# Masked softmax on one core: contiguous first halves, a new order of the last masks and divides, and batch 14 stored in two parts

## The chip, the cores and the metric

The kernel runs on one core of one Trainium2 chip. The metric is the device time of one execution in microseconds (us). All executions quoted here ran at a granted clock of 1.0. Differences of a few tenths rest on several rounds and carry a 95% interval.

## The reference

For each of 16 batches (8 heads x 256 queries = 2048 rows of 256 float32), softmax over the first `length` columns; the others are zero. Lengths are drawn between 128 and 255.

```python
for b in range(batch):
    length = lengths[b]
    masked = x[b, :, :, :length].copy()
    masked = masked - np.max(masked, axis=-1, keepdims=True)
    exp_masked = np.exp(masked)
    result[b, :, :, :length] = exp_masked / np.sum(exp_masked, axis=-1, keepdims=True)
```

## The kernel before

A batch is 2 MB, held as 128 partitions x 16 rows x 256 columns; eight batches have a slot in SBUF. VectorE masks a batch by a minimum in place, ScalarE takes exponentials with row sums, VectorE divides each half (8 of the 16 rows of every partition), the sync queue (SP) stores. Batches 0 to 3 are loaded whole by SP; batches 4 to 15 by GpSimd (POOL), cut to the batch's length rounded up to one of twelve widths.

```python
x_f = x.rearrange("b h q k -> b (h q) k").rearrange("b (p t) k -> b p t k", p=P)
...
for h in range(2):                                    # batch 0, in halves
    s = slice(h * half, (h + 1) * half)
    nc.sync.dma_start(out=xt[:, 0, s], in_=x_f[0, :, s]).then_inc(s_ld[h], 16)
for b in range(1, ahead):                             # batches 1 to 3
    nc.sync.dma_start(out=xt[:, b], in_=x_f[b]).then_inc(s_ld[b + 1], 16)

nc.sync.wait_ge(s_exp, 3)
for b in range(batch):
    s_b = s_st[b % 2]
    for s in parts(b):
        nc.sync.wait_ge(s_out, 2 * b + (s.stop - 1) // half + 1)   # divided
        if b >= 2 and s.start == 0:
            nc.sync.wait_ge(s_b, 64 * (b // 2 + 1))                # store b-2 has landed
        nc.sync.dma_start(
            out=out_f[b, :, s, :], in_=xt[:, b % slots, s, :]
        ).then_inc(s_b, 16 * ((s.stop - s.start) // quarter))
...
for b in range(batch):                                # VectorE
    first = b == 0 or b >= ahead
    if first:
        divide(b, 0)
    if b + 1 < batch:
        mask(b + 1, slice(0, nt))
    if not first:
        divide(b, 0)
    divide(b, 1)
```

Each half of batch 0 is thus 128 pieces of 8 KB at a pitch of 16 KB in memory. Batches 13 and 14 are stored in one piece of 2 MB, batch 15 in two of 1 MB.

The softmax here doesn't subtract the row's maximum and nothing guards it: scores larger than these inputs give would overflow.

## Time and profile before

| | before |
|---|---|
| median of 3 runs | 156.60 us (156.06 to 156.62) |
| span of the profiled run | 154.7 us |
| VectorE busy, ScalarE busy | 75%, 68% |
| 16 transfer engines busy, both queues | 97.9% |
| bytes moved | 62.08 MB, 401 GB/s over the span |
| traffic, start of the first load packet to start of the last packet | 2.1 to 152.7 us |

A line of the view by stretches gives the stretch (us from the start), its length, the busy time of five engines with their number of instructions, then the granted clock, the mean busy share of the 16 transfer engines, and GB/s. It counts a packet whole in the stretch in which the packet starts, so that a share can pass 1. A line of the timeline gives start, duration, engine, source line, operation, tiles, and in brackets how long the engine had been idle and for whom. A line of the waits gives who waited for whom: total us, times, longest. The lines of this kernel stand in the prediction.

### The profile page before, as it was taken

What the parts mean: (1) busy time and instruction counts of PE and PEld (TensorE: products, weight loads), DVE (VectorE), ACT (ScalarE), POOL (GpSimd) and SP (SyncE); (2) the same over time, 40 slices, a digit from 0 to 9 for tenths busy, and PEclk for the clock granted to TensorE, in tenths of its full rate; (3) what the DMA queues carried; (4) which work ended last, traced back from release to release, by engine and by line L of the source; (5) the groups of instructions that cost most, each with busy time, mean ns of one, the idle gap of its engine ahead of it and who ended that gap; (6) DMA issues with size and microseconds to landing.
All of it is one profiled execution on the core that took longest, in us unless ns stands there. A gap on an engine that the chain in (4) does not pass through costs nothing.

```text
span 154.7 us, 1324 instructions
## 1 busy us (share of the span) xinstructions
PE 0.2 (0%) x1; PEld 0.1 (0%) x1; DVE 115.7 (75%) x84; ACT 105.2 (68%) x514; POOL 19.0 (12%) x25
## 2 busy tenths in 40 slices
PE   0000000000000000000000000000000000000000
PEld 0000000000000000000000000000000000000000
DVE  1249999952999696979979696969689629796700
ACT  3087799992692959778695959595976906959200
POOL 4910031000220110201111020202001000000000
DMA  4999999999999999999999999999999999999992
GB/s 116 426 449 424 428 398 406 398 407 447 400 410 395 402 409 414 415 417 411 404 424 407 417 408 409 415 416 416 416 417 419 419 448 415 426 445 419 430 421 85
DMA packets 9988, 62.08 MB, mean 401 GB/s; under 512 B 850, under 2 KB 946, under 8 KB 6274
## 3 DMA queue, kind: packets, MB, share of 16 engines
q1 hardware_dynamic: 5904, 41.95, 65.8%
q0 software_dynamic: 4080, 20.12, 32.1%
q14 instruction: 2, 0.02, 0.0%
q10 hardware_dynamic: 2, 0.00, 0.0%
HBM read 28.51 MB, written 33.55 MB: 401 GB/s over the span
## 4 chain that ended last, share of the span: by engine, by line
DMA 55%; DVE 19%; ACT 8%; issue 8%; ACTq 2%; SPq 1%; POOLq 1%; DVEq 0%
DMA xt<-in_x_dram 34%; DMA out_dram<-xt 21%; DVE xt L222 9%; DVE xt L195 9%; ACT xt L252 8%; ACTq L252 2%; DVE inv_sum L219 1%; SPq L109 1%; POOLq L99 0%; SPq L111 0%; SPq L120 0%; DVEq L212 0%; POOLq L135 0%; POOLq L130 0%; ACTq L247 0%
## 5 line engine op out<-in xcount | busy, mean ns | idle before, releaser
L252 ACT ACTIVATE xt<-xt x256 | 102.4, 401 | 37.2 <-DVE xt L195 37.2
L222 DVE TENSOR_TENSOR xt<-xt,inv_sum 128x2048 f32<-128x2048 f32 x32 | 73.4, 2292 | 1.1
L252 ACT ACTIVATION_READ_ACCUMULATOR xt<-xt x256 | 47.9, 187 | 0.0
L195 DVE SCALAR_TENSOR_TENSOR xt<-down,len_s,xt 128x2048 f32<-128x2048 f32 (+1 forms) x17 | 37.8, 2222 | 13.1 <-DMA xt<-in_x_dram 13.0
L130 POOL DMA_DIRECT2D xt<-in_x_dram x12 | 12.8, 1064 | 95.5 <-issue 50.6
L219 DVE RECIPROCAL inv_sum<-row_sum 128x8 f32<-128x8 f32 x32 | 6.3, 198 | 14.4 <-ACT xt L252 14.4
L149 POOL MEMSET xt<- 128x1536 f32 x4 | 5.3, 1386 | 1.1 <-DVE len_s L186 1.1
L244 ACT ACT_TABLE_LOAD x1 | 1.3, 1283 | 1.6 <-SPq L81 1.6
L178 DVE TENSOR_SCALAR down<-iota_i 128x256 f32<-128x256 int32 x1 | 0.3, 297 | 1.6 <-POOL iota_i L141 1.6
L183 DVE CAST len_b<-word 1x16 bf16<-1x16 int32 x1 | 0.2, 163 | 0.4 <-DMA word<-in_lengths_dram 0.4
L186 DVE TENSOR_SCALAR len_s<-len_f 128x16 f32<-128x16 f32 x1 | 0.2, 174 | 0.3 <-PE len_f L165 0.3
L141 POOL IOTA iota_i<- 128x256 int32 x1 | 0.3, 331 | 0.6 <-SPq L81 0.6
L146 POOL MEMSET seed<- 1x1 f32 x2 | 0.3, 162 | 0.0
L244 ACT ACTIVATE warm<-const-float32-0.0 128x1 f32<-128x1 f32 x1 | 0.2, 203 | 0.0
L144 POOL MEMSET ones<- 1x128 bf16 x1 | 0.2, 194 | 0.0
L165 PE MATMUL len_f<-len_b,ones 1*128 1x16 bf16 x1 | 0.2, 164 | 2.6 <-DVE len_b L183 2.6
L275 POOL MEMSET const-float32-0.0<- 128x1 f32 x1 | 0.1, 98 | 0.3 <-issue 0.3
L165 PEld LDWEIGHTS len_f<-len_b,ones 1*128 1x128 bf16 x1 | 0.1, 99 | 2.6 <-POOL ones L144 2.6
L275 POOL MEMSET const-float32-1.0<- 128x1 f32 x1 | 0.1, 98 | 0.0
L275 POOL MEMSET const-bfloat16-1.0<- 128x1 bf16 x1 | 0.1, 98 | 0.0
L275 POOL MEMSET const-uint8-127<- 128x1 uint8 x1 | 0.1, 98 | 0.0
L275 POOL BASE_LOAD x1 | 0.0, 17 | 0.1
## 6 DMA issues: line engine op xcount, KB each, us to landing
out_dram<-xt SPq DMA_DIRECT2D x19, 1024.0 KB
out_dram<-xt SPq DMA_DIRECT2D x14, 512.0 KB
xt<-in_x_dram SPq DMA_DIRECT2D x3, 2048.0 KB, 16.1
out_dram<-xt SPq DMA_DIRECT2D x3, 2048.0 KB
xt<-in_x_dram POOLq DMA_DIRECT2D x3, 1728.0 KB, 16.9
xt<-in_x_dram POOLq DMA_DIRECT2D x2, 2048.0 KB, 18.5
xt<-in_x_dram POOLq DMA_DIRECT2D x2, 1600.0 KB, 16.8
xt<-in_x_dram POOLq DMA_DIRECT2D x2, 1280.0 KB, 14.8
```

What stands on the lines that cost most here:

```text
L109: nc.sync.dma_start(out=xt[:, 0, s], in_=x_f[0, :, s]).then_inc(s_ld[h], 16)
L130: nc.gpsimd.dma_start(out=xt[:, slot, :, :w], in_=x_n[:, n, :, :w]).then_inc(s_sw[par], 16)
L141: nc.gpsimd.iota(iota_i, pattern=[[1, seq_k]], base=0, channel_multiplier=0).then_inc(s_iota, 1)
L146: nc.gpsimd.memset(seed[:, par : par + 1], 0.0).then_inc(s_st[par], 64)
L149: nc.gpsimd.memset(xt[:, b, :, low:], 0.0).then_inc(s_fill, 1)
L165: nc.tensor.matmul(len_f, lhsT=ones, rhs=len_b, start=True, stop=True).then_inc(s_lenf, 1)
L195: return nc.vector.scalar_tensor_tensor(out=t, in0=down[:, None, lo:hi].to_broadcast([P, s.stop - s.start, hi - lo]), scalar=len_s[:, b : ...
L219: step(nc.vector.reciprocal(out=inv_sum[:, b, s], in_=row_sum[:, b, s]))
L222: nc.vector.tensor_tensor(out=t, in0=t, in1=inv_sum[:, b, s, None].to_broadcast([P, half, seq_k]), op=ALU.mult,).then_inc(s_out, 1)
L244: nc.scalar.activation(out=warm, in_=nc.const_aps.tensor(0.0, (P, 1), F32), func=EXP)
L252: ins = nc.scalar.activation(out=e, in_=e, func=EXP, accum_out=sum_h[:, bass.ds(i, 1), j])
L275: nc = _bacc.Bacc("TRN2", target_bir_lowering=False, num_devices=1)
```

## The change

It means to make the first loads quicker (each half of batch 0 one contiguous megabyte), to let the divide of 13's second half go ahead while VectorE waits for batch 14's load, to have the last mask done before the divides of 14 so that ScalarE isn't kept waiting for it, and to start batch 14's store half a batch earlier.

```diff
+    x_0 = x[0].rearrange("h q k -> (h q) k").rearrange("(u p t) k -> p u t k", u=2, p=P)
+    out_0 = out[0].rearrange("h q k -> (h q) k").rearrange("(u p t) k -> p u (t k)", u=2, p=P)
...
-        elif b < 13 or b == batch - 1:
+        elif b != batch - 3:
             cuts = [0, half, nt]
...
-            nc.sync.dma_start(out=xt[:, 0, s], in_=x_f[0, :, s]).then_inc(s_ld[h], 16)
+            nc.sync.dma_start(out=xt[:, 0, s], in_=x_0[:, h]).then_inc(s_ld[h], 16)
...                                        (batch 0 is stored to out_0 to match)
-            first = b == 0 or b >= ahead
-            if first:
-                divide(b, 0)
-            if b + 1 < batch:
-                mask(b + 1, slice(0, nt))
-            if not first:
-                divide(b, 0)
-            divide(b, 1)
+            at = 0 if b == batch - 2 else 2 if b == batch - 3 else 1 if b == 0 or b >= ahead else 0
+            for h in range(3):
+                if h == at and b + 1 < batch:
+                    mask(b + 1, slice(0, nt))
+                if h < 2:
+                    divide(b, h)
```

More of the change, by code (lines that the diff above doesn't have):

```diff
@@ L119 @@
                     nc.sync.wait_ge(s_b, 64 * (b // 2 + 1))
-                nc.sync.dma_start(
-                    out=out_f[b, :, s, :], in_=xt[:, b % slots, s, :]
-                ).then_inc(s_b, 16 * ((s.stop - s.start) // quarter))
+                if b == 0:
+                    to = out_0
+                    at = xt[:, b, s, :].rearrange("p (u t) k -> p u (t k)", u=2)
+                else:
+                    to = out_f[b, :, s, :]
+                    at = xt[:, b % slots, s, :]
+                nc.sync.dma_start(out=to, in_=at).then_inc(s_b, 16 * ((s.stop - s.start) // quarter))
         def pick(v, n, slot, par, ws):
```

## The prediction

> **What bounds the kernel now.** I read, in this order, the first two parts of the page, its DMA queues, the stretches of the span at the start and the end, the waits of the store queue, and the timeline of the last 28 us. The lines of the page:
>
> ```profile
> PE 0.2 (0%) x1; PEld 0.1 (0%) x1; DVE 115.7 (75%) x84; ACT 105.2 (68%) x514; POOL 19.0 (12%) x25
> ...
> DMA  4999999999999999999999999999999999999992
> GB/s 116 426 449 424 428 398 406 398 407 447 400 410 395 402 409 414 415 417 411 404 424 407 417 408 409 415 416 416 416 417 419 419 448 415 426 445 419 430 421 85
> ...
> q1 hardware_dynamic: 5904, 41.95, 65.8%
> q0 software_dynamic: 4080, 20.12, 32.1%
> ```
>
> No compute engine is above 75% of the span, while the 16 transfer engines are at nine tenths or more in every slice but the first and the last. The two queues' shares add up to 97.9%. The bytes are 62.08 MB; nothing in the change alters them. Traffic runs from 2.0 us to 152.7 us, so 62.08 MB / 150.7 us = 412 GB/s. The time is that stretch, plus 2.0 us ahead of the first packet, plus 2.0 us after the last one (the span is 154.7 us), plus 1.7 us between the span and the timed 156.37 us of the same run. A change therefore gains only where it (a) starts the traffic sooner or makes it denser, (b) fills a hole in it, or (c) shortens the run-out. The chain of waits puts 55% on DMA, but much of its rest is compute that merely lies beside busy queues, so I don't size the change from it.
>
> The stretches at the two ends (us, engines' busy time, granted clock, DMA share, GB/s):
>
> ```profile
> 147.00:147.50 0.50, 0.00 (x0) 0.00 (x0) 0.00 (x0) 0.00 (x0) 0.00 (x0) 1.00 0.89 377
> 150.50:151.00 0.50, 0.00 (x0) 0.00 (x0) 0.00 (x0) 0.00 (x0) 0.00 (x0) 1.00 1.04 442
> 151.25:151.50 0.25, 0.00 (x0) 0.00 (x0) 0.00 (x0) 0.00 (x0) 0.00 (x0) 1.00 0.55 229
> 151.75:152.00 0.25, 0.00 (x0) 0.00 (x0) 0.00 (x0) 0.00 (x0) 0.00 (x0) 1.00 0.24 98
> 152.50:152.75 0.25, 0.00 (x0) 0.00 (x0) 0.00 (x0) 0.00 (x0) 0.00 (x0) 1.00 0.08 33
> ```
>
> The queues are full to 151.25 us; then three or four of the 16 engines run on alone for 1.4 us at the same pace each (98 GB/s at a share of 0.24, 0.24 x 16 = 3.8 engines, 26 GB/s each; all 16 at 430 GB/s are 27 each). So the end belongs to the slowest engines, and their pace does not depend on what the others do.
>
> The last vector instructions and the last load's issue and landing time:
>
> ```profile
> 126.58 2.35 DVE L195 SCALAR_TENSOR_TENSOR xt<-down,len_s,xt 128x2048 f32<-128x2048 f32 x1 [3.29 <-DMA xt<-in_x_dram]
> 137.56 0.42 ACT L252 ACTIVATE xt<-xt  x1 [1.88 <-DVE xt L195]
> 144.33 2.29 DVE L222 TENSOR_TENSOR xt<-xt,inv_sum 128x2048 f32<-128x2048 f32 x1
> ```
> ```profile
> xt<-in_x_dram POOLq DMA_DIRECT2D x1, 2048.0 KB, 17.6
> ```
>
> Counting the instructions back from the end, 126.58 is the mask of 14, 129.08 the second divide of 13, 132.75 the first of 14, 134.97 the mask of 15, 137.46 the second divide of 14, 141.13 and 144.33 the divides of 15. ScalarE idles 1.88 us waiting for the mask of 15, and VectorE 3.29 us before the mask of 14. The last load was issued at 116.06 us and landed 17.6 us later, at 133.7.
>
> The store queue's waits, from 135 to 140 us and from 140 to 144 us:
>
> ```profile
> SPq L119 <- DMA out_dram<-xt: 4.5, 1, 4.5
> SPq L120 <- DVE xt L222: 1.0, 1, 1.0
> ```
> ```profile
> SPq L119 <- DMA out_dram<-xt: 3.6, 1, 3.6
> ```
>
> Its issues are at 133.81 (store 13), 139.78 (14), 143.77 (first half of 15) and 146.65 us (second half). Stores 13 and 15 wait for an older store to land (each waits for the store two batches back), store 14 for store 12 and then 1.0 us more for its divide, and only the very last half for compute alone.
>
> **What the Trainium skill says.** *DMA: Bandwidth & Descriptors*, "Where 436 GB/s comes from", puts the ceiling of one core's 16 ports at 435 GB/s; the plain loads here run at 430 GB/s from 9 to 20 us, so there is hardly anything above them. The same page, "Queues, rings and completion order", says that each engine goes round its queues packet by packet; the trace agrees: from 126 to 128 us both queues pass 36 packets, and the one with the larger packets takes 69% of the time. The same page, "Latency and other measured facts", tells of a slow row pitch from 512 KiB upward. Batch 0's halves have a pitch of 16 KiB, far below that; the trace neither shows nor excludes a small effect at this pitch. *HBM Reference*, "Specifications", says that a core streaming alone is bounded by its 16 DMA engines, which is what the run-out above shows.
>
> **The change part by part.**
>
> *Batch 0's halves contiguous.* Each half is still 128 pieces of 8 KB; only the pitch goes from 16 KB to 8 KB. The stretches of 1 us show 180, 319, 401 and 410 GB/s from 2 to 6 us. Against 430 that is 250 + 111 + 29 + 20 = 410 KB short, or 0.95 us. The 250 KB of the first microsecond are start-up (every engine's first packet, with the share already at 0.87), which the pitch does not touch; I leave them. The remaining 160 KB are 0.37 us, the most that better addresses can give back. Nothing shows that the pitch is the cause: the second half, at the same old pitch, runs at 442 and 492 GB/s. I choose half of it, **0.2 us**. It would go through in full, since the queues are busy ever after.
>
> *Store 0* becomes 256 pieces of 8 KB in place of 128 of 16 KB, and batch 14's two halves likewise, with 16 completion packets more: 128 + 128 + 16 = 272 packets, 17 per engine. From 134 to 146 us packets of 8 and 16 KB together moved 5.26 MB in 12 us, 438 GB/s, no less than the 16 KB loads' 430. I take **0**, at most 0.1 us. With smaller packets in store 0, load 4 gets a larger share beside it and lands earlier than its 37.4 us; stores land later by as much, and the bytes stay.
>
> *The order on VectorE.* No instruction is added. The mask of 14 goes behind both divides of 13. VectorE is free at 123.3, the second half's exponentials end at 129.18 - 5.27 = 123.9, so that divide fills the 3.29 us hole: 123.9 + 0.2 + 2.3 = 126.4, and the mask of 14 starts at about 126.6 as before. Store 13 is ready 5 us sooner, but it is held for store 11 until 133.8 us anyway. Then the mask of 15 waits for its load, 133.7 us, and ends at 136.1. The divides of 14, ready at 132.5, now stand behind it: 136.1 to 138.6 and to 140.9. ScalarE's second half of 14 ends at 135.7, so its hole shrinks from 1.88 to about 0.6 us; exponentials of 15 to 139.6 and 142.9; divides of 15 to 143.3 and 145.6. The last one ends at 145.6 in place of 146.6, **1.0 us sooner**.
>
> *Where that second goes.* First half of 14: issued when store 12 has landed, 138.7, in place of 139.78. First half of 15: still held for store 13, 143.8. Last half: 145.6. All of it is queued behind work that the slowest engines have not done: at 146.65, 2.1 MB, some 5 us, are still to move in the old kernel. So the last packet stays where it is. The dips to 0.87 to 0.93 between 146 and 148 us, 0.2 us of all engines, may fill, but they should be the fast engines' dips. I count **0.1 us**.
>
> Sum: the three runs' mean 156.4, minus 0.2, minus 0.1: **156.1 us**.
>
> **The rivals.** *First: the tail's compute sets the end,* and the whole 1.0 us arrives, perhaps with some more from finer stores: 155.0 to 155.4. For it: the last store is issued by a divide (2.5 us wait), and the share dips there. Against: 2.1 MB of backlog and a share back at 1.0 until 151. *Second: the pitch matters more than I think* and the start gains 0.5 to 0.9 us: 155.5 to 155.9. For it: 382 GB/s from 2 to 9 us against 430 after. Against: the second half's rate. *Third: the mask of 15 in front becomes a wait.* If its load lands later than 133.7, since store 13's early readiness or a changed phase of the queues shifts it, both divides of 14 slip. The order has about 1 us of room before the last divide is as late as it was, and some 4 us of backlog behind that; only a slip of over 3 us would show, as 157 or more. *Fourth: everything hidden:* 156.4.
>
> **Range and chances.** The old runs differ by 0.56 us, more than my gain. The low end, 155.3, allows for one of the first two rivals in most part, the high end, 156.8, for no gain with the slower of the runs. Two per cent are 3.1 us: three times the sum of what start and tail could give, so faster gets 0.01; slower needs a stall that the backlog can't cover, 0.01; within 2% 0.98.
>
> **What would show it.** The bytes and the two queues' shares should be the same, with about 272 more packets on q1. From 3 to 6 us, a rate over 420 GB/s would mean that the pitch was the cause; about 377 that it was not. VectorE's last divide should end near 145.6, its hole before the mask of 14 should shrink below 1 us, and a new one of about 4 us stand before the mask of 15. The last packets should still end 150.7 us after the first, with three or four engines alone at the end. If the stretch from first to last packet has shrunk by a microsecond, the engines were not continuously busy and I am wrong; if the mask of 15 starts after 137 us, the third rival holds.

## The result, and the profile after

The changed kernel takes 156.41 us (median of 6 runs, 156.34 to 156.47); the kernel before, in the same rounds and its first three runs together, 156.53 us (155.87 to 156.64). The ratio is 1.0002, with an interval of 0.9982 to 1.0021: no difference. All ratios here are the mean time of one kernel's fast runs over that of the other's of the same rounds, so not quite the ratio of the medians.

The page of the changed kernel, the same rows as before:

```profile
DMA  3999999999999999999999999999999999999992
GB/s 114 430 438 445 419 358 393 418 409 433 421 404 390 411 406 417 412 416 410 407 424 406 411 414 411 413 410 415 418 418 420 419 441 419 423 440 419 426 428 116
...
q1 hardware_dynamic: 6176, 41.95, 65.9%
q0 software_dynamic: 4080, 20.12, 32.1%
```

Same bytes, same shares, and 6176 - 5904 = 272 packets more on the sync queue. The transfer engines are as full as they were.

The end, in the view by stretches:

```profile
147.00:147.50 0.50, 0.00 (x0) 0.00 (x0) 0.00 (x0) 0.00 (x0) 0.00 (x0) 1.00 1.05 442
150.50:151.00 0.50, 0.00 (x0) 0.00 (x0) 0.00 (x0) 0.00 (x0) 0.00 (x0) 1.00 1.05 442
151.25:151.50 0.25, 0.00 (x0) 0.00 (x0) 0.00 (x0) 0.00 (x0) 0.00 (x0) 1.00 1.08 459
151.75:152.00 0.25, 0.00 (x0) 0.00 (x0) 0.00 (x0) 0.00 (x0) 0.00 (x0) 1.00 0.56 230
152.50:152.75 0.25, 0.00 (x0) 0.00 (x0) 0.00 (x0) 0.00 (x0) 0.00 (x0) 1.00 0.15 66
```

The dip of the old kernel at 147 us (0.89) is filled. But the quick engines are merely done with other work at another time; the last packet starts at 152.8 us, against 152.7 before. After 152 us the share is between 0.08 and 0.16, so one to three engines are left, not quite the three or four foretold.

VectorE and ScalarE, from the timeline:

```profile
127.13 2.35 DVE L203 SCALAR_TENSOR_TENSOR xt<-down,len_s,xt 128x2048 f32<-128x2048 f32 x1
134.43 2.35 DVE L203 SCALAR_TENSOR_TENSOR xt<-down,len_s,xt 128x2048 f32<-128x2048 f32 x1 [4.96 <-DMA xt<-in_x_dram]
...
144.25 2.29 DVE L230 TENSOR_TENSOR xt<-xt,inv_sum 128x2048 f32<-128x2048 f32 x1
```
```profile
137.04 0.42 ACT L259 ACTIVATE xt<-xt  x1 [0.82 <-DVE xt L203]
```

The order does what it is meant to: the 3.29 us hole before the mask of 14 is gone, and ScalarE's wait for the mask of 15 shrinks from 1.88 to 0.82 us. In their place VectorE waits 4.96 us for the last load, with both divides of 14 behind it. The last divide ends at 146.54 us, against 146.62 before.

That pair of profiles hides a gain, because the issue of the last load moves from profile to profile: over the ten of normal start and bytes it lies between 114.54 and 117.40 us, in either order. In the repeat of the changed kernel (below) it comes early, and the last divide ends at 144.47 us:

```profile
114.54 0.56 POOL L138 DMA_DIRECT2D xt<-in_x_dram  x1 [9.32 <-DMA out_dram<-xt]
132.36 2.35 DVE L203 SCALAR_TENSOR_TENSOR xt<-down,len_s,xt 128x2048 f32<-128x2048 f32 x1 [4.98 <-DMA xt<-in_x_dram]
...
142.18 2.29 DVE L230 TENSOR_TENSOR xt<-xt,inv_sum 128x2048 f32<-128x2048 f32 x1
```

From the issue of the last load to the end of the last divide it is 30.5 to 30.6 us in all five profiles with the old order, and 29.9 to 30.0 us in the five with the new one and no extra pass. So the order does end compute 0.6 us sooner, counted from that load.

The store queue's waits from 136 to 139 us and from 143 to 150 us:

```profile
SPq L123 <- DMA out_dram<-xt: 4.4, 1, 4.4
```
```profile
SPq L293 <- DMA out_dram<-xt: 5.9, 1, 5.9
SPq L130 <- DVE xt L230: 2.4, 2, 2.1
SPq L123 <- DMA out_dram<-xt: 1.6, 1, 1.6
```

The stores are issued at 134.05 (13), 139.25 and 141.69 (14), 144.13 and 146.57 us (15); before: 133.81, 139.78, 143.77 and 146.65. After the last issue the queue waits 5.9 us for what is still to land, against 5.8 before.

The start:

```profile
2.00:3.00 1.00, 0.17 (x1) 0.10 (x1) 0.34 (x2) 0.99 (x2) 0.00 (x0) 1.00 0.78 164
3.00:6.00 3.00, 0.00 (x0) 0.00 (x0) 0.00 (x0) 0.14 (x1) 2.96 (x3) 1.00 0.94 393
```

Before, these two stretches had 180 and 377 GB/s. So 164 + 3 x 393 = 1343 KB in place of 180 + 3 x 377 = 1311 KB: 32 KB or 0.08 us, under half of the 0.2 us that I had counted, and within the scatter of the table further down. The first store is nonetheless issued at 19.61 us, 0.25 us sooner.

### The profile page after: what moved, and what is told of

Same layout as the page of the kernel before. It is cut to its first block, busy times and chain, and to the rows that moved or that the text cites. A ratio compares the mean times of both kernels' runs of the same rounds, so it can differ in the third digit from the quotient of the medians.

```text
span 154.8 us, 1325 instructions
## 1 busy us (share of the span) xinstructions
PE 0.2 (0%) x1; PEld 0.1 (0%) x1; DVE 115.7 (75%) x84; ACT 105.2 (68%) x514; POOL 19.0 (12%) x25
## 3 DMA queue, kind: packets, MB, share of 16 engines
q1 hardware_dynamic: 6176, 41.95, 65.9%
## 4 chain that ended last, share of the span: by engine, by line
DMA 64%; DVE 19%; issue 5%; ACT 2%; SPq 2%; POOLq 1%; ACTq 1%; DVEq 0%
DMA xt<-in_x_dram 43%; DMA out_dram<-xt 20%; DVE xt L230 12%; DVE xt L203 6%; ACT xt L259 2%; SPq L130 1%; DVE inv_sum L227 1%; ACTq L259 1%; SPq L113 1%; POOLq L103 0%; POOLq L138 0%; SPq L115 0%; POOLq L143 0%; DVEq L220 0%; POOLq L161 0%
```

## The experiments

My theory: the transfer engines set the time from the first to the last packet; only bytes, their rate and the start count, and the end of compute has slack. The first rival: the last divides set the end. The second: the two parts of the change each do something and cancel. The third: a lead at the start is lost on the way. "Before" in each ratio is the kernel before in the same rounds on the same chip.

**The contiguous start alone** (the changed kernel with order and `parts` as before).

> The kernel before with batch 0's load halves and store contiguous, nothing of the tail. Transfer theory (the start's gain goes through): 0.1 to 0.3 us faster than the kernel before, ratio 0.998 to 0.9995. Rival (the lead is lost on the way, since a lead of 0.25 us in the first store was gone by 52 us in the changed kernel): ratio 1.000, with the first store issued at 19.6 us all the same. Rival (the parts cancel): over 0.4 us faster here, and the tail alone slower by as much.

Measured: 155.98 us against 156.19, ratio 0.9985 (0.9968 to 1.0003). It leans to a gain, but the interval holds 1. The first store was issued at 19.50 us.

**The new tail alone** (the kernel before with the new order and batch 14 in halves).

> The kernel before with the new order on VectorE and batch 14 in halves, the start as before. Transfer theory: ratio 1.000, within 0.15 us; the first store at 19.86 us; VectorE waits 4 to 5 us ahead of the mask of 15. Rival (tail compute sets the end): 0.3 to 1 us faster or, if the wait for the last load hurts, slower by as much.

Measured: 156.23 us against 156.19, ratio 1.0000 (0.9982 to 1.0017), the first store at 19.82 us and a wait of 4.95 us ahead of the mask of 15. The tail neither gives nor takes anything that this interval, some 0.3 us to either side, could show; a tenth would not be seen.

**One more pass ahead of the last divide**.

```diff
+            if b == batch - 1 and h == 1:
+                step(nc.vector.tensor_tensor(out=spare, in0=t,
+                    in1=inv_sum[:, b, s, None].to_broadcast([P, half, seq_k]), op=ALU.mult))
+                nc.vector.wait_ge(s_v, v)
```

> The changed kernel with one more VectorE pass of 2.29 us ahead of the very last divide, so the last half store is issued at about 148.9 us in place of 146.57. Transfer theory: the last half has until about 149.2 us (queues empty of other work at 150.2, less 0.9 us from issue to first packet as at the start), so 0 to 0.3 us longer. Rival (the last divide sets the end): 2.3 us longer.

Measured: 156.19 us against 156.19, ratio 1.0004 (0.9983 to 1.0025). The last store was issued at 149.27 us, 2.7 us later than in the changed kernel's own profile, and nothing came of it. The stretches show how:

```profile
149.00:150.00 1.00, 0.00 (x0) 0.00 (x0) 0.25 (x1) 0.00 (x0) 0.00 (x0) 1.00 0.22 90
150.00:151.00 1.00, 0.00 (x0) 0.00 (x0) 0.00 (x0) 0.00 (x0) 0.00 (x0) 1.00 0.96 401
151.00:152.00 1.00, 0.00 (x0) 0.00 (x0) 0.00 (x0) 0.00 (x0) 0.00 (x0) 1.00 0.98 401
152.00:152.50 0.50, 0.00 (x0) 0.00 (x0) 0.00 (x0) 0.00 (x0) 0.00 (x0) 1.00 1.22 508
152.50:152.75 0.25, 0.00 (x0) 0.00 (x0) 0.00 (x0) 0.00 (x0) 0.00 (x0) 1.00 0.03 0
```

From 149 to 150 us most engines stand still, a hole of 0.78 of a microsecond over all sixteen; then all of them work to 152.5 us and stop together, with no run-out but a single packet at 152.76 us. The hole costs nothing because it lies in the quick engines: in the changed kernel they wait for the slow ones at the very end, here they wait a little earlier. This is the plainest evidence that a few slow engines, not the mean of the sixteen, set the end. Which ones they are the trace doesn't say.

**Two more passes.** The same edit, twice.

> The changed kernel with two more VectorE passes ahead of the very last divide (4.6 us). Transfer theory with its slack now used up: in the run with one pass the queues stood nearly empty from 149 to 150 us and the end did not move, so all of the second pass is paid for: 2.0 to 2.5 us longer than before, 1.013 to 1.016. Rival (some other bound lies at the end, so that even this is hidden): under 0.5 us. Rival (every pass counts): 4.6 us.

Measured: 158.23 us against 156.13, ratio 1.0104 (1.0059 to 1.0148). The medians differ by 2.1 us, as expected; the ratio, which rests on few runs, is below the expected 1.013, though its interval reaches it. Three of the four runs lie between 158.17 and 158.42, the fourth at 156.83, which I can't explain (its trace was not taken). The last store of the profiled run was issued at 151.55 us:

```profile
150.00:151.00 1.00, 0.00 (x0) 0.00 (x0) 1.00 (x1) 0.00 (x0) 0.00 (x0) 1.00 0.08 33
151.00:152.00 1.00, 0.00 (x0) 0.00 (x0) 0.53 (x1) 0.00 (x0) 0.00 (x0) 1.00 0.00 0
...
154.00:155.00 1.00, 0.00 (x0) 0.00 (x0) 0.00 (x0) 0.00 (x0) 0.00 (x0) 1.00 0.82 336
```

Now all engines are empty for a microsecond and more: a hole that is paid for. From its issue until nearly all engines are done, the last megabyte takes 3.2 us (149.27 to 152.5 with one pass; 151.55 to about 154.8 with two). The changed kernel's last packet is at 152.8, so its last store could be issued as late as about 149.6: by this estimate **the last divide has about 3 us of slack**. The kernel before should have about as much (its last store is issued at 146.65 us); there it was not tried. This is why neither shortening nor reordering the end of compute shows.

**Fewer bytes, no less compute.** Of batch 7's two last quarters one row in four is stored; the result is wrong (the other three stay unwritten).

```diff
+                if b == 7 and s.start > 0:
+                    r = slice(s.start, s.start + 1)
+                    to = out_f[b, :, r, :]
+                    at = xt[:, b % slots, r, :]
```

> The changed kernel, but of batch 7's two last quarters only one row in four is stored (a wrong result on purpose): 786 KB less in the middle of the run, no compute less. Transfer theory: 786 KB / 412 GB/s = 1.9 us shorter. Rival (compute or waits set the end): 0 to 0.5 us shorter.

Measured: 154.38 us against 156.19, ratio 0.9875 (0.9852 to 0.9898); 1.25% of 156.2 is 1.95 us, against the 1.9 of 786 KB at 412 GB/s. The transfers in the middle of the run are paid for in full.

**A late start.** SP's first load waits until VectorE has prepared the lengths.

```diff
+        nc.sync.wait_ge(s_v, 2)
         for h in range(2):
```

> The changed kernel, but the sync queue's first load waits for VectorE's preparation of the lengths (3.0 us), so all traffic starts 1.9 us later. Transfer theory: a shift of the first packet goes through in full, 1.8 to 2.0 us longer. Rival (a lead or lag of the start is taken up on the way, as the changed kernel's lead of 0.25 us seemed to be): under 1 us longer.

Measured: 158.08 us against 156.13, ratio 1.0125 (1.0094 to 1.0156), or 1.95 us. The first load was issued at 3.02 us in place of 1.13, 1.89 us later. So a lag of the first packet reaches the end in full. This speaks against a loss on the way, but a true lead was not tested: the contiguous start makes hardly any lead in bytes.

**The pitch, four times over.** First the kernel before with batches 1 to 3 in strided halves too:

```diff
-            nc.sync.dma_start(out=xt[:, b], in_=x_f[b]).then_inc(s_ld[b + 1], 16)
+            for h in range(2):
+                s = slice(h * half, (h + 1) * half)
+                nc.sync.dma_start(out=xt[:, b, s], in_=x_f[b, :, s]).then_inc(s_ld[b + 1], 16)
```

> The kernel before, with batches 1 to 3 loaded in strided halves like batch 0 (8 KB pieces at a pitch of 16 KB), so four times the strided bytes. Pitch theory: 370 to 410 GB/s from 8 to 20 us in place of 430, and 0.5 to 1.1 us longer than before. Rival (pitch of no account, the low rate from 3 to 6 us is start-up): 425 to 435 GB/s there, ratio 1.000.

Then the contiguous start with batches 1 to 3 in contiguous halves (`in_=x_u[b][:, h]`, the analogue of `x_0`, and stores to match):

> The kernel with the contiguous start alone, and batches 1 to 3 loaded in contiguous halves of 1 MB too (8 KB pieces, pitch 8 KB), stores to match. Control for the run before: piece size 8 KB without the pitch. Pitch theory: 0.5 to 1.1 us shorter than the strided one; rival: the same within 0.2 us. If both are slower than the kernel before, the 8 KB pieces cost something, against my 0.

Measured: 156.36 us, ratio 1.0022 (1.0003 to 1.0041) for the strided one; 156.35 us, ratio 1.0017 (0.9993 to 1.0041) for the contiguous one. The two agree, and so do their rates from 8 to 20 us, by the stretches of the strided and of the contiguous one:

```profile
8.00:20.00 12.00, 0.00 (x0) 0.00 (x0) 9.59 (x7) 9.91 (x49) 0.38 (x1) 1.00 1.01 426
```
```profile
8.00:20.00 12.00, 0.00 (x0) 0.00 (x0) 9.91 (x7) 10.03 (x51) 0.38 (x1) 1.00 1.01 425
```

With pieces of 16 KB it is 430 in the kernel before. So a pitch of 16 KB shows no cost against contiguous memory. Smaller pieces may cost up to 1%, which over those 12 us would be 0.1 us, but the kernels with 16 KB pieces scatter too (430 before, 425 with the contiguous start alone), so that stays open.

**The start alone, and the whole change, once more on one chip.**

> The contiguous start alone once more, beside the whole change on one chip. If the start gains about 0.2 us on its own (first time 0.9985, interval 0.9968 to 1.0003), 0.9985 to 0.999 again; if that was chance, 1.000.

> The whole change once more, on the same chip as the start alone. If the tail takes nothing, as in the run of the tail alone (1.000), the same ratio as the start alone within 0.15%; if the tail's part takes the gain back, 0.15% more.

Measured: start alone 156.22 us, ratio 1.0011 (0.9992 to 1.0031); whole change 156.21 us, ratio 1.0017 (0.9994 to 1.0039); before 156.00 us. The start's first lean to a gain did not come back: its two results, 0.9985 and 1.0011, average 0.9998. Neither part does anything that these intervals can show, so nothing needs to cancel. On this chip all four kernels came out 0.1 to 0.2% over the kernel before, the strided one's interval just clear of 1; nothing of the kind stood on the first chips for the start or for the whole change, and I read nothing into it. The profiled run of the whole change was this time its shortest, 155.73 us, beside 157.01 us for its longest: one and the same kernel differs by over a microsecond on one chip.

Over all profiles but those of the late start and the narrow loads, the start looks like this (GB/s; the first three rows are strided, the others contiguous):

| kernel | 2 to 3 us | 3 to 6 us | KB, 2 to 6 us | first store issued |
|---|---|---|---|---|
| before | 180 | 377 | 1311 | 19.86 |
| tail alone | 197 | 393 | 1376 | 19.82 |
| all strided | 197 | 377 | 1328 | 19.90 |
| changed kernel | 164 | 393 | 1343 | 19.61 |
| start alone, first and second run | 147, 115 | 401, 404 | 1350, 1327 | 19.50, 19.58 |
| one pass, two passes | 147, 123 | 404, 391 | 1359, 1296 | 19.52, 19.64 |
| changed kernel again | 156 | 404 | 1368 | 19.45 |
| all contiguous | 180 | 391 | 1353 | 19.59 |
| fewer bytes | 131 | 399 | 1328 | 19.50 |

The means are 1338 KB in the three strided profiles and 1340 KB in the eight contiguous ones. On average the contiguous start has a slower first microsecond (145 against 191 GB/s) and three quicker ones after it (398 against 382), the same bytes by 6 us. What does differ is the first store, 0.2 to 0.4 us sooner in every contiguous run. It seems to be a matter of when data lands rather than of how much moves, which I did not trace further; as the engines are full either way, nothing comes of it.

**Fewer bytes with a right result: narrower loads for batches 1 to 3.** The run with fewer bytes points here. GpSimd loads these batches at their own width (240, 232 and 256 of 256 columns).

```diff
-        for b in range(1, ahead):
-            nc.sync.dma_start(out=xt[:, b], in_=x_f[b]).then_inc(s_ld[b + 1], 16)
...
+        for b in range(1, ahead):
+            nc.gpsimd.memset(xt[:, b, :, low:], 0.0).then_inc(s_fill, 1)
+            ...
+            v_len = length(POOL, word[0:1, 2 * b : 2 * b + 1])
+            nc.gpsimd.wait_ge(s_fill, b)
+            pick(v_len, bass.ds(b, 1), bass.ds(b, 1), s_ld[b + 1], widths + [seq_k])
```

> The changed kernel, with batches 1 to 3 loaded from GpSimd's queue at their own width (240, 232 and 256 of 256 columns for these lengths) in place of whole rows: 40 columns less, 2048 rows x 40 x 4 B = 0.33 MB less, right results. Transfer theory: 0.33 MB / 412 GB/s = 0.8 us shorter than the changed kernel if the queue stays fed at the start, ratio to before 0.994 to 0.996. Rival (GpSimd issues batch 1 too late, after the first 2 MB are through at 7 us, or more small rows are slower): 0 to 2 us longer.

Measured: 158.60 us against 156.13, ratio 1.0136 (1.0110 to 1.0163): a miss. The bytes are down to 61.76 MB as meant. But look at the stretches and at the queues from 12 to 16 us:

```profile
12.00:16.00 4.00, 0.00 (x0) 0.00 (x0) 1.69 (x1) 2.32 (x12) 4.00 (x4) 1.00 1.01 319
...
80.00:120.00 40.00, 0.00 (x0) 0.00 (x0) 34.08 (x25) 30.59 (x153) 5.17 (x5) 1.00 1.02 414
```
```profile
q0 software_dynamic: 291, 1.28, 101.3%
```

The engines are full, so the queue was fed in time, yet they move only 319 GB/s. The rows here are of 928 and 960 bytes, in packets of 1.28 MB / 291 = 4.4 KB, and nothing else is in flight. It isn't the queue as such. From 21 to 23 us, still before the first store (23.14 us), the same queue carries mostly batch 3, whose whole rows go in packets of 16 KB, and the rate is back:

```profile
21.00:23.00 2.00, 0.00 (x0) 0.00 (x0) 1.00 (x1) 2.00 (x12) 0.00 (x0) 1.00 1.04 430
```

Later, beside stores in large pieces, narrow loads go along at 414 GB/s in all. From 8 to 20 us the loss is about 110 GB/s x 12 us = 1.3 MB, or 3.1 us; less the 0.8 us saved, 2.3 us are left. The medians differ by 2.5 us; the ratio amounts to 2.1 us. But the profiled run was the slowest of the eight, 160.11 us, so some 1.6 us of its own excess stay unexplained. So bytes are the currency only at an equal rate. No kernel was found that beats both.

## Why the prediction was right

**The bound.** Right: fewer bytes saved 1.95 us for 1.9 worked out, a later start cost 1.95 us for 1.89, and 2.7 us of later compute cost nothing.

**The slowest engines own the end.** Right, and borne out by the profile with one more pass: a hole of 0.78 us that only the quick engines had, and no run-out afterwards.

**The order on VectorE.** The mechanism was right: hole before the mask of 14 filled, a wait of 4.96 us (foretold: about 4) before the mask of 15, ScalarE's wait down to 0.82 us (about 0.6). Wrong was the size of the term "1.0 us sooner" for the last divide. In the one pair of profiles it was 0.08 us, because the last load happened to be issued 0.58 us later than in the trace before (116.64 against 116.06 us). Counted from that issue, the order gained 0.6 us: the mask of 15 began 17.8 us after it, not the 17.6 at which the load lands, and the spacing of reciprocal and divide, 2.44 us each time, takes another 0.2 us. A wait for a transfer has to be counted from that transfer's issue, which moved by up to 2.9 us between profiles. Had the second arrived, the 3.0 us of slack would have swallowed it.

**The backlog behind the tail.** I gave "some 4 us of backlog" behind the last divide, and about 3 us as the slip that would show. By the runs with one and two passes it is about 3 us; the larger figure was too much. The "2.1 MB, some 5 us" from which it came still holds the last megabyte itself.

**The start.** This term failed. "I choose half of it, 0.2 us" was to be the gain of the better pitch. Over all profiled runs the contiguous start moves the same bytes by 6 us (1340 against 1338 KB), and the start alone has ratios of 0.9985 and 1.0011. The rate from 3 to 6 us went to between 391 and 404, neither the 420 that was to prove the pitch nor the 377 that was to refute it; the strided tail-alone profile had 393 too, so this sign couldn't decide. What I had left out is the first microsecond, where the contiguous runs lose, on average, what they gain later.

**The tail's 0.1 us** for the dips between 146 and 148 us: the dip at 147 us did fill, but the tail alone has a ratio of 1.0000, with an interval too wide for a tenth. It was rightly said that they should be the quick engines' dips, and then a tenth should not have been counted for them.

The time was near the forecast and in its range, but that says little: the range, 155.3 to 156.8 us, held no gain as well. The gain at the start was not there, and that of the tail can't be seen; the better forecast was the fourth rival, everything hidden.

## What to carry to other kernels

Here, with the transfer queues full from end to end, reordering compute was worth nothing that could be measured, and delaying it cost time only once every engine stood empty; a pass of delay ahead of the last store measures that slack in one run. Count a gain at the start in bytes moved by a given time, not in when the first data lands. And before cutting bytes with narrower rows, see at what rate such rows move when nothing else is in flight.

## What the Trainium skill lacked or had wrong

- The Trainium skill's *DMA: Bandwidth & Descriptors*, "Specifications", gives 512 B as the smallest transfer for line rate. Rows of 928 to 960 B on GpSimd's queue, alone in flight, moved at 319 GB/s with the engines full, against 430 for packets of 16 KB on the same queue; only beside large stores was the sum 414.
- The same page, "Latency and other measured facts", has row pitches from 512 KiB up and nothing below (and at 512 KiB itself hardly a loss: 207 GB/s, where it calls 214 full). Pieces of 8 KB at a pitch of 16 KB ran at 426 GB/s from 8 to 20 us, contiguous ones at 425.
- That section also calls two of the engines, 7 and 15, usually slower. None that I read says what uneven engines do to the end of a kernel: here one to four of the sixteen ended up to 1.4 us after the others (which ones the trace doesn't say), so a hole of 0.78 us in the quick ones cost nothing, and the mean busy share of the sixteen did not show that slack.
